# Quarters 1 to 3 of the first x block moved ahead of a runtime branch, in a macaron FFN, attention and convolution layer on 8 cores

## The chip, the cores and the metric

The kernel runs on all 8 cores of one Trainium2 chip. The time is the device time of the slowest core in microseconds (us), the median of the fast runs of a kernel. In some executions of any version the cores of one die (cores 0 to 3 or 4 to 7), sometimes of both, show a lower granted clock and the time is 2 to 19% longer; such runs are of the slow state and are left out of medians, means and ratios. "Same" is the class for a difference under 2%. Numbers of single cores come from profiled executions.

The program holds two bodies. The even cores (0, 2, 4, 6) run the first, by falling through a branch on a register; the odd cores (1, 3, 5, 7) take the branch to the second. An even core and the odd one after it are called a pair here.

## The reference, cut to what matters

Input x is 4 x 4096 x 1024, float32.

```python
def reference(x, ...):
    x = x + 0.5 * swiglu(rmsnorm(x, ffn1_norm), gate1, up1, down1)   # d_ff 2816
    z = rmsnorm(x, mix_norm) @ w_in                   # q, k, v (8 heads of 64) | a, b (512 each)
    attn = chunk_band_attention(q, k, v, rel_bias)    # 64-frame chunks, 576-key band
    conv = swish(layernorm(depthwise_conv31(a * sigmoid(b)) + dw_bias))
    x = x + concat(attn, conv) @ w_out
    x = x + 0.5 * swiglu(rmsnorm(x, ffn2_norm), gate2, up2, down2)
    return rmsnorm(x, final_norm)
```

(The comments are this text's shorthand.) Each core holds its share of the frames and works in two groups, group 0 and group 1, each through the whole layer.

## The kernel before

The kernel is written as a list scheduler: helpers such as `P.dma` append instructions and the waits they need to one list for each engine; the lists are replayed at the end. Estimated durations decide only the order.

The start. `load_x(G[0], 0, 4, some=...)` loads block 0 of x in quarters of 512 KB on the sync engine's queue:

```python
P.t["sp"] = 1.0
load_x(G[0], 0, 4, some=(0,))
P.dma("sp", lambda h: h.dma_start(out=cs[:, 0:CS_N], in_=cs_d), "cs0", ...)
P.first = P.E["sp"].items[:]          # what is in here goes out ahead of the branch
del P.E["sp"].items[:]
P.t["sp"] = 4.0
load_x(G[0], 0, 4, some=(1, 2, 3))    # in the body, behind the branch
tk = ("xl0_0_1", 16, "dma")           # quarter 1 has landed
P._need("pool", tk)                   # the gate: GpSimd's weight loads wait for it
for s, parts, m in ((2, 2, 2), (1, 4, 1)):
    issue_weights(ws["next"] + m)
    load_x(G[0], s, parts, eng="pool")
issue_weights()
# ... cut ...
for it in progs[0].first:
    it[1](nc.sync).then_inc(sems[it[2]], 16)
second = nc.values_load(half_d)
with nc.If(second == 0):
    body(progs[0])                    # even cores
with nc.Else():
    body(progs[1])                    # odd cores
```

The way of the convolution's input through HBM, in two halves r = 0 and 1 for each group. In the profile these are the store `gscr_0<-dreg` (group 1: `gscr_1<-dreg`) and the reload `dreg<-gscr_0`:

```python
def to_phases(g, r):
    P.dma("sp", ... out=gs_d[gi][r], in_=gTs[gi][:, r] ..., reads=(("g", gi, r),), writes=(("gs", gi, r),))
    P.dma("sp", ... out=gps[gi] ..., in_=gs_d[gi][r], reads=(("gs", gi, r),), ...)
    F.add(("gp", gi, r))
    hold["keys"] = (("gp", gi, m * r),)   # weight loads issued from here on wait for the reload
```

The softmax here doesn't subtract the row's maximum and nothing guards it: scores larger than these inputs give would overflow.

Of the kernel before, what the change touches and what calls it, by code (L numbers as in the profile page):

```python
# [283 lines left out]
def build_nc(debug=None):  # L284
# [20 lines left out]
    with ExitStack() as es:  # L305
# [81 lines left out]
        def make(half):  # L387
            P = Prog()
            plan = PLANS[half]
            G = [Group(i, b) for i, b in enumerate(plan)]  # L390
# [312 lines left out]
            def load_x(g, s, parts=1, eng="sp", some=None):  # L703
                n, c0 = g.n[s], g.off[s]
                w = 8 // parts
                for i in range(parts) if some is None else some:
                    lo, hi = 8 * c0 + i * w * n, 8 * c0 + (i + 1) * w * n
                    src = xin_d[g.gi, :, lo:hi]
                    wk = tuple(("x", g.gi, k, s) for k in range(i * w, (i + 1) * w))
                    P.dma(eng, lambda h, src=src, lo=lo, hi=hi: h.dma_start(out=xres[:, lo:hi], in_=src),  # L710
                          "xl%d_%d_%d" % (g.gi, s, i), 512 * w * n, writes=wk)
                F.add(("x", g.gi, s))
                if some == (0,):
                    return
                S.add(0, norm_load(g, s))
# [887 lines left out]
            P.t["sp"] = 1.0  # L1603
            load_x(G[0], 0, 4, some=(0,))
            P.dma("sp", lambda h: h.dma_start(out=cs[:, 0:CS_N], in_=cs_d), "cs0", 512 * CS_N, writes=("cs",), issue=0.45)
            P.first = P.E["sp"].items[:]
            del P.E["sp"].items[:]
            P.t["sp"] = 4.0
            load_x(G[0], 0, 4, some=(1, 2, 3))
            tk = ("xl0_0_1", 16, "dma")  # L1610
            P._need("pool", tk)
            P.t["pool"] = P.fin[tk[0:2]]
# [29 lines left out]
            return P  # L1642

        progs = [make(0), make(1)]
        sems = {}
        for nm in sorted(set(progs[0].sem_names()) | set(progs[1].sem_names())):
# [152 lines left out]
```

## Time and profile before

| | before |
|---|---|
| time | 1324.84 and 1324.96 us |
| spans, even cores 0, 2, 4, 6 | 1321.8, 1321.7, 1321.5, 1323.3 us |
| spans, odd cores 1, 3, 5, 7 | 1318.0, 1317.3, 1317.3, 1318.3 us |
| PE busy on core 6 | 1292.1 us, 98% |

The page of core 6 (the slowest), its busy time and the shares of the chain of work that ended last:

```profile
PE 1292.1 (98%) x8666; PEld 740.4 (56%) x8666; DVE 487.1 (37%) x899; ACT 407.0 (31%) x727; POOL 229.0 (17%) x266
...
PE 92%; DVE 3%; DMA 2%; issue 1%; ACT 1%; SPq 0%; DVEq 0%; POOL 0%; ACTq 0%; POOLq 0%
```

The kernel is bound by PE.

The chain of waits at the start of core 6 (start in us, duration, what; SPq is the sync engine's sequencer, L1673 its register load for the branch):

```profile
1.98 1.86 SPq L1673
...
4.47 3.73 DMA xres<-xin
...
8.81 7.63 DMA ring<-wgu
...
16.57 8.68 PE psA L561 x32
```

Read it downwards: quarters 1 to 3 of x go out only at 4.47 us, because the register loads stand in front of them; GpSimd's gate opens when quarter 1 has landed; the first weights need 7.63 us from issue to landing; then PE starts. The timeline of the same core has the same points as instructions (start, duration, engine, line, operation, tiles, count, and in brackets the idle time before and who ended it):

```profile
4.47 1.28 SPq L710 DMA_DIRECT2D xres<-xin  x3
...
8.81 2.29 POOL L668 DMA_DIRECT2D ring<-wgu  x4 [8.11 <-DMA xres<-xin]
...
16.57 5.23 PE L561 MATMUL psA<-dreg,ring 128*128 128x512 bf16 x16 [2.49 <-DMA ring<-wgu]
```

Here and below, a matmul is called warm when TensorE's granted clock is 1.00 and cold when it is near 0.5. This tile ran cold in part: its 16 matmuls took 5.23 us at a granted clock of 0.62 (16 to 18 us) and 0.53 (18 to 20 us), where core 0's took 3.62 us. PE had idled 2.49 us before it.

What the DMA engines of the two cores of a pair did at 8 to 10 us (the table of windows: the length of the stretch, then busy time and count of PE, PEld, DVE, ACT and POOL; the last three columns are the granted clock, the busy share of the core's 16 DMA engines and GB/s). Core 6 first, then core 7:

```profile
8.00:10.00 2.00, 2.00 (x11) 1.17 (x10) 1.16 (x3) 1.27 (x3) 1.19 (x2) 1.00 0.99 377
```

Core 1's timeline shows how late an odd core begins: GpSimd, ScalarE and VectorE execute the branch at 2.65 to 2.8 us (PE at 3.8, the sync engine at 4.3), but the first instruction of the body starts at 7.1, and x goes out then:

```profile
7.11 0.17 DVE L1602 MEMSET cb_sb<- 128x128 bf16 x1 [7.11 <-issue]
7.16 2.45 SPq L710 DMA_DIRECT2D xres<-xin  x3
...
13.69 2.58 POOL L668 DMA_DIRECT2D ring<-wgu  x4 [12.98 <-DMA xres<-xin]
```

Two loads of convolution weights go out at 311.14, the second store of the conv input at 311.86; the store has landed when its reload is issued, at 321.75:

```profile
311.14 1.08 POOL L668 DMA_DIRECT2D ring<-cwscr  x2 [27.13 <-DMA dreg<-gscr_0]
...
311.86 0.37 SPq L1080 DMA_DIRECT2D gscr_0<-dreg  x1
...
321.75 0.32 SPq L1085 DMA_DIRECT2D dreg<-gscr_0  x1
321.78 0.61 DVE L1295 TENSOR_TENSOR dreg<-ps,cs_sb 128x432 f32<-128x432 f32 x1 [3.82 <-PE ps L561]
...
322.54 1.89 PE L561 MATMUL ps<-at,hT 128*128 128x512 bf16 x8 [0.77 <-DVE dreg L1295]
```

VectorE's idle time is put down to PE, the last releaser by the record; but it starts 0.03 us after the reload is issued, so the store's landing released it. PE then idles 0.77 us.

### The profile page before, as it was taken

To read this page: it belongs to the slowest core of one execution; us is meant where nothing else is said; L and a number is where in the kernel's file an instruction comes from. 1 tells how busy PE (TensorE), PEld (TensorE's weight loads), DVE (VectorE), ACT (ScalarE), POOL (GpSimd) and SP (SyncE) were. 2 spreads that over 40 slices of the span, in tenths; PEclk is the share of its full clock that TensorE was granted. 3 is DMA by queue.
4 is the path that set the end of the run, shared out by engine and by line. 5 is a ranking of instruction groups with operands and counts; after the bars stand their busy time and mean duration, and the time that the engine had idled before them with its cause. 6 is when DMAs were issued, how large, how long until landed. Compare 5 with 4: busy or idle time off the path is not lost.

```text
span 1323.3 us, 23324 instructions; the slowest of 8 cores (1317.3 to 1323.3 us)
## 1 busy us (share of the span) xinstructions
PE 1292.1 (98%) x8666; PEld 740.4 (56%) x8666; DVE 487.1 (37%) x899; ACT 407.0 (31%) x727; POOL 229.0 (17%) x266
## 2 busy tenths in 40 slices
PE   7999999999999999999999999999999999999995
PEld 3655655566665666665564444446566664444444
DVE  4522222263745522222266222125455362222125
ACT  3411011242666421001236110114338661101123
POOL 2263000341003320000161000014120220000022
PEclk9999999999999999999999999999999999999998
DMA  8795226244930753243445844342784125433503
GB/s 187 164 217 116 49 47 120 42 127 142 193 70 2 188 91 72 53 76 53 73 52 101 218 80 82 66 76 49 171 208 103 34 39 111 75 65 64 112 0 130
DMA packets 33923, 129.55 MB, mean 98 GB/s; under 512 B 2832, under 2 KB 13200, under 8 KB 26896
## 3 DMA queue, kind: packets, MB, share of 16 engines
q0 software_dynamic: 18752, 97.33, 38.9%
q1 hardware_dynamic: 15056, 30.68, 6.8%
q8 instruction: 73, 1.20, 0.4%
q14 instruction: 42, 0.34, 0.1%
HBM read 193.54 MB, written 18.68 MB: 160 GB/s over the span
## 4 chain that ended last, share of the span: by engine, by line
PE 92%; DVE 3%; DMA 2%; issue 1%; ACT 1%; SPq 0%; DVEq 0%; POOL 0%; ACTq 0%; POOLq 0%
PE psA L561 53%; PE ps L561 39%; DVE hT L823 1%; DMA gscr_1<-dreg 1%; DMA ring<-wgu 1%; DVE xres L1048 1%; DVE xres L823 0%; DMA dreg<-gscr_1 0%; ACT L569 0%; DMA xres<-xin 0%; ACT rstd L574 0%; SPq L1673 0%; DVE xres L1556 0%; ACT pb L574 0%; POOL ssb L771 0%
## 5 line engine op out<-in xcount | busy, mean ns | idle before, releaser
L561 PE MATMUL psA<-hT,ring 128*128 128x512 bf16 (+2 forms) x3792 | 691.4, 344 | 1.7 <-DVE dreg L1139 1.0
L561 PEld LDWEIGHTS psA<-hT,ring 128*128 128x128 bf16 x3792 | 370.6, 98 | 316.1 <-issue 3.6
L574 ACT ACTIVATE dreg<-psA 128x512 f32<-128x512 f32 (+3 forms) x279 | 162.3, 587 | 688.1 <-PE psA L561 678.6
L561 PE MATMUL ps<-at,ring 128*128 128x512 bf16 (+2 forms) x1920 | 326.6, 332 | 0.0
L1014 DVE TENSOR_TENSOR at<-psA,dreg 128x512 bf16<-128x512 f32 (+2 forms) x213 | 130.1, 612 | 450.7 <-PE psA L561 427.3
L561 PEld LDWEIGHTS ps<-at,ring 128*128 128x128 bf16 x1920 | 187.6, 98 | 137.2
L1048 DVE SCALAR_TENSOR_TENSOR xres<-ps,xres 128x512 f32<-128x512 f32 (+2 forms) x160 | 88.5, 556 | 168.0 <-PE ps L561 168.0
L766 POOL TENSOR_TENSOR ssum<-ssum,sq 128x512 f32<-128x512 f32 (+2 forms) x102 | 103.2, 1012 | 169.4 <-ACT sq L574 165.6
L668 POOL DMA_DIRECT2D ring<-wgu x47 | 25.6, 546 | 522.9 <-PE ps L561 261.0
L561 PE MATMUL ps<-dreg,ring 128*128 128x256 bf16 (+4 forms) x704 | 85.7, 274 | 2.1 <-DMA dreg<-gscr_1 1.5
L574 ACT ACTIVATE sq<-xres 128x256 bf16<-128x256 f32 (+2 forms) x108 | 55.3, 519 | 99.8 <-DVE xres L1048 66.7
L823 DVE SCALAR_TENSOR_TENSOR hT<-xres,cs_sb,rstd 128x256 bf16<-128x256 f32 (+2 forms) x120 | 70.4, 644 | 12.4 <-ACT rstd L574 12.4
L561 PEld LDWEIGHTS ps<-dreg,ring 128*128 128x128 bf16 x704 | 55.2, 98 | 23.1 <-issue 4.4
L561 PE MATMUL ps<-hT,ring 128*128 128x512 bf16 (+2 forms) x352 | 63.4, 336 | 0.0
L561 PEld LDWEIGHTS ps<-hT,ring 128*128 128x128 bf16 x352 | 33.6, 98 | 25.5 <-issue 0.4
L569 ACT ACT_TABLE_LOAD x36 | 46.2, 1283 | 0.6
L574 ACT ACTIVATE pb<-psA 128x1024 bf16<-128x1024 f32 (+2 forms) x42 | 37.7, 915 | 8.1 <-PE psA L561 7.9
L1556 DVE TENSOR_TENSOR xres<-ps,xres 128x256 f32<-128x256 f32 (+2 forms) x48 | 24.9, 531 | 37.2 <-PE ps L561 37.1
L1576 POOL TENSOR_TENSOR dreg<-pb 128x2560 bf16<-128x2560 bf16 x8 | 35.8, 4502 | 0.7 <-DMA cwscr<-dreg 0.7
L668 POOL DMA_DIRECT2D ring<-wdA x16 | 8.6, 537 | 135.7 <-PE psA L561 135.3
L561 PE MATMUL ps<-at,hT 128*128 128x512 bf16 x136 | 30.8, 379 | 0.0
L561 PE MATMUL psA<-cb_sb 64*128 64x64 bf16 (+3 forms) x456 | 27.8, 223 | 0.0
(93 smaller groups left out, 588.5 us busy)
## 6 DMA issues: line engine op xcount, KB each, us to landing
ring<-wgu POOLq DMA_DIRECT2D x41, 1024.0 KB, 8.4
ring<-wdA POOLq DMA_DIRECT2D x16, 768.0 KB, 8.6
ring<-wdB POOLq DMA_DIRECT2D x16, 640.0 KB, 7.9
ring<-cwscr POOLq DMA_DIRECT2D x16, 640.0 KB, 9.7
cwscr<-dreg SPq DMA_DIRECT2D x8, 640.0 KB, 6.1
ring<-wab POOLq DMA_DIRECT2D x8, 512.0 KB, 8.2
ring<-wout POOLq DMA_DIRECT2D x4, 1024.0 KB, 14.7
dreg<-xin SPq DMA_DIRECT2D x2, 2048.0 KB, 21.9
```

Of the source, the lines that this page charges most:

```text
L561: P.op("pe", lambda h: h.matmul(o, lhsT=lhsT, rhs=rhs, start=start, stop=stop, skip_group_check=True), (max(n / 2400.0 + 0.0025, 0.03) if ...
L569: P.op("act", lambda h: h.activation(out=cs[0:1, CS_N + i:CS_N + i + 1], in_=onesS[0:1, 0:1], func=func), 1.5, ("cb1",), ())
L574: P.op("act", lambda h: h.activation(out=out, in_=in_, func=func, **kw), 0.12 + n / 1200.0 + (0.09 * sum(isinstance(v, bass.AP) for v in k ...
L668: P.dma("pool", lambda h, dst=dst, src=src: h.dma_start(out=dst, in_=src), wtok(p, i), (256 if p.reads else 512) * w, reads=p.reads, after ...
L766: pool(lambda h: h.tensor_tensor(out=ss, in0=ss, in1=sqt, op=ALU.add), n, (sk, ("sq", i)), (sk,))
L823: dve(lambda h, dst=dst, xin=xin, gcol=gcol: h.scalar_tensor_tensor(out=dst, in0=xin, scalar=gcol, in1=rt, op0=ALU.mult, op1=ALU.mult), n, ...
L1014: dve(lambda h: h.tensor_tensor(out=at, in0=ub, in1=tt, op=ALU.mult), n, (("ps", bU), ("tmpF", ti)), (("AT", gi, fl, s),))
L1048: dve(lambda h, xo=xo, xi=xi, bk=bk: h.scalar_tensor_tensor(out=xo, in0=bk, scalar=0.5, in1=xi, op0=ALU.mult, op1=ALU.add), n, (("ps", b), ...
L1556: dve(lambda h, xo=xo, bk=bk: h.tensor_tensor(out=xo, in0=bk, in1=xo, op=ALU.add), n, (("ps", b),) + rk, (("x", gi, dm, s),))
L1576: P.op("pool", lambda h, o_=o_, i0=i0: h.tensor_tensor(out=o_, in0=i0, in1=i1, op=ALU.mult), 4.5, ("cmp", "ic", "cb"), (("cwb", i % 2),))
```

## The change

Its intent: the sync queue is empty while the register loads and the branch run, so give it all of block 0 first. The gate stays on quarter 1.

```diff
             load_x(G[0], 0, 4, some=(0,))
             P.dma("sp", lambda h: h.dma_start(out=cs[:, 0:CS_N], in_=cs_d), "cs0", ...)
+            load_x(G[0], 0, 4, some=(1, 2, 3))
             P.first = P.E["sp"].items[:]
             del P.E["sp"].items[:]
             P.t["sp"] = 4.0
-            load_x(G[0], 0, 4, some=(1, 2, 3))
             tk = ("xl0_0_1", 16, "dma")
             P._need("pool", tk)
```

Both bodies share what is ahead of the branch, so the odd cores issue their x early as well.

## The prediction

> **What bounds the kernel now.** The page gives PE 98% busy and a chain of waits that is 92% PE: only the first tens of microseconds can move. The even cores take 1321.5 to 1323.3 us (core 6 is slowest), the odd ones 1317.3 to 1318.3: the even cores set the time.
>
> The start on core 6, by timeline and chain: the sync engine issues quarter 0 of x block 0 at 1.07 us and the constants at 1.52, spends 1.86 + 0.47 us on register loads, and issues quarters 1 to 3 only at 4.47. Quarter 0 lands at 5.0, quarter 1 at 8.2, quarter 3 about 11.2. GpSimd waits for quarter 1 (8.1 us) and issues the first weights at 8.81; their first half lands 7.63 us later, and the first real tile starts at 16.57, after 2.5 us of PE idling on that DMA. From there PE is nearly full, except where that GpSimd queue feeds it late (core 0: third weight piece at 32.4 us).
>
> In core 6's DMA records the hardware queue moves about 0.4 MB per us, and nothing from about 5 to 6 us: the hole that the change fills.
>
> **What the change does.** No work is added or removed. Three issues (1.28 us of the sync queue) move from 4.47 to about 2.0 us, before the branch. The sync engine branches 1.3 us later, which costs nothing (next task at 41 us); GpSimd loads its branch register itself.
>
> With the queue kept busy, quarter 1 lands at about 6.2 us (estimate: 1.1 MB at 0.4 MB per us from 2.0 us, plus about 1 us of latency and landing), quarter 3 at about 8.5. So the gate opens 2.0 to 2.5 us sooner on even cores, and the weight stream moves with it. Odd cores enter the branch at 6.6 to 7.9 us ([...] the trace has instruction packets there), quarter 1 lands at 13.1, and they gain 4 to 5 us, off the path.
>
> Given back: the odd weight stream starts about 2 us after the even one instead of 4.5, and while both run an even core's weights arrive at about 0.15 instead of 0.2 MB per us; that costs 0.5 to 0.8 us (estimate).
>
> The statistics of block 0 become bound by ScalarE (1.24 us per quarter) instead of DMA and end about 1.2 us earlier, so PE idles about 1.5 us before the first tile. [...] I expect it warm, which saves core 6 up to 1.6 us more.
>
> **Sum.** Even cores gain 1.5 us, core 6 about 2.5 to 3. Slowest span about 1320.7 us; time about 1322.8 us, range 1321.0 to 1324.8. Faster by over 2%: 1%; within 2%: 98%; slower: 1%.
>
> **What would show it.** Quarter 1's landing and the first weight issue at 6 to 7 us on even cores (8.81 before); first tile at 14.2 to 14.8 us in 3.6 us; odd cores ending 4 us sooner; the same instructions, apart from a few warm-up matmuls.
>
> **What would make it wrong.** x in flight holding up the odd cores' instruction fetch by several us; a cold first tile on some even core (+1.6 us); pair contention taking the whole shift, so that core 0 still waits for its third weight piece at 32 us; a schedule in another order; slow-state runs.

2.0 to 2.5 us at the gate less 0.5 to 0.8 us given back make about 1.5 us on the even cores, and core 6 adds up to 1.6 us (5.23 - 3.62), which was put at 2.5 to 3 in all. The trace of the kernel before has the numbers behind the estimates: 377 to 414 GB/s on cores 6 and 0 at 8 to 10 us; 1.02 us from core 6's first issue of x (1.07) to its first packet (2.09); and on core 6, while GpSimd loaded weights, 211 GB/s at 16 to 18 us and 152 to 164 at 18 to 24, when core 7 got 145 to 156.

## More of the kernel before

The convolution's accumulation, whose target lies over the buffer that the second store (r = 1) still reads, so that it waits for that store (L1295 in the profile of core 0's convolution stage of group 0):

```python
dve(lambda h, ...: h.tensor_tensor(out=a3, in0=b3, in1=bc, op=ALU.add), w, (("ps", b), "cs"), ak)
```

The convolution weights (`ring<-cwscr`, eight pieces of 640 KB for each group) come through GpSimd's queue.

```profile
8.00:10.00 2.00, 2.00 (x11) 1.35 (x10) 0.79 (x2) 1.25 (x3) 0.00 (x0) 1.00 0.55 111
```

Core 6 has its DMA engines nearly always busy and gets 377 GB/s, while its neighbour has just begun and gets 111.

## The result, and the profile after

| | before | changed kernel |
|---|---|---|
| median of the fast runs (3 and 4) | 1324.84 us (1323.6, 1324.84, 1324.96; one slow run, 1436.27, left out) | 1326.12 us (1324.52, 1325.28, 1326.95, 1329.01) |
| ratio of fast runs | | 1.0015, 95% interval 0.9991 to 1.0039: same |
| spans, even cores 0, 2, 4, 6 | 1321.8, 1321.7, 1321.5, 1323.3 | 1323.0, 1327.0, 1318.7, 1322.6 |
| spans, odd cores 1, 3, 5, 7 | 1318.0, 1317.3, 1317.3, 1318.3 | 1317.6, 1320.2, 1321.3, 1320.6 |

A ratio here is the mean time of one kernel's fast runs over that of the other's fast runs of the same rounds, so it is not quite the ratio of the medians quoted.

The time is in the predicted class, but outside the predicted range, on the side of no gain. And the even cores, which agreed within 2 us before, now spread over 8 us. The page of core 2, the slowest, has the chain nearly as before, with DMA at 3% instead of 2%:

```profile
PE 91%; DMA 3%; DVE 3%; issue 1%; ACT 1%; DVEq 0%; POOL 0%; SPq 0%; ACTq 0%; POOLq 0%
```

**The start of an even core.** The chain of waits at the start of core 6, then its timeline:

```profile
1.99 6.82 DMA xres<-xin
```

```profile
1.99 1.52 SPq L710 DMA_DIRECT2D xres<-xin  x3
...
9.42 2.31 POOL L668 DMA_DIRECT2D ring<-wgu  x4 [8.72 <-DMA xres<-xin]
...
15.18 3.61 PE L561 MATMUL psA<-dreg,ring 128*128 128x512 bf16 x15 [0.26 <-DMA ring<-wgu]
```

Quarters 1 to 3 go out 2.5 us sooner, as planned, but quarter 1 takes 6.82 us instead of 3.73, and the gate opens at 9.42 instead of 8.81. (The whole block is no sooner either: on the even cores its last quarter lands at 11.6 to 12.0 us, against 11.0 to 11.3 before.) PE still starts 1.4 us sooner on this core, warm, since from the weights' issue to the tile it takes 5.8 us (15.18 - 9.42) instead of 7.8 (16.57 - 8.81). Why the weights were faster is not shown; two things fit: when they went out, 0.46 MB of this core's x were still to land instead of 0.65, and the neighbour's x had landed by 12.6 us instead of 15.8. The windows of core 6 and then of core 7, 8 to 10 us, show why quarter 1 was slow:

```profile
8.00:10.00 2.00, 2.00 (x9) 1.02 (x7) 1.09 (x2) 1.71 (x3) 0.58 (x1) 1.00 0.94 287
```

```profile
8.00:10.00 2.00, 0.00 (x0) 0.00 (x0) 0.00 (x0) 0.00 (x0) 0.00 (x0) 1.00 0.96 291
```

Now both cores of the pair load at once, with their DMA engines about as busy (0.94 and 0.96), and core 6 gets 287 GB/s instead of 377, core 7 291. Over 4 to 6 us it was 277 and 243, over 6 to 8 us 242 and 152.

**The start of an odd core.** The chain of waits of core 1, then its timeline:

```profile
3.00 7.39 issue
...
10.41 3.69 issue
```

```profile
1.98 1.90 SPq L710 DMA_DIRECT2D xres<-xin  x3
10.50 0.17 DVE L1602 MEMSET cb_sb<- 128x128 bf16 x1 [10.50 <-issue]
...
14.10 2.29 POOL L668 DMA_DIRECT2D ring<-wgu  x4 [13.39 <-issue]
```

x goes out 5 us sooner than before, but the body starts 3.4 us later, at 10.50, and the first weights go out at 14.10 with "issue" ahead of them: nothing that the profile shows was waited for. GpSimd executed its branch at 2.95 us. What lies between fits its instruction fetch: in the raw DMA records the first packets of core 1's instruction queues after the start come at 4.3 us before the change and at 8.5 after it, when 1.3 of the 2.2 MB of x and constants have landed. On the even cores, which fall through the branch, there are none before 33.0 us in either kernel.

**The convolution stage of core 0**, the lines that answer to those shown above, and the chain's view of it:

```profile
308.56 1.08 POOL L668 DMA_DIRECT2D ring<-cwscr  x2 [25.86 <-PE psA L561]
...
310.55 0.37 SPq L1080 DMA_DIRECT2D gscr_0<-dreg  x1
...
321.64 0.32 SPq L1085 DMA_DIRECT2D dreg<-gscr_0  x1
321.67 0.61 DVE L1295 TENSOR_TENSOR dreg<-ps,cs_sb 128x432 f32<-128x432 f32 x1 [5.02 <-DMA gscr_0<-dreg]
...
322.43 2.48 PE L561 MATMUL ps<-at,hT 128*128 128x512 bf16 x8 [1.96 <-DVE dreg L1295]
```

```profile
310.55 11.03 DMA gscr_0<-dreg
```

The core came here 1.3 us sooner than before and left no sooner: the store takes 11.03 us instead of 9.9, PE idles 1.96 us instead of 0.77, and the 8 matmuls behind the gap take 2.48 us instead of 1.89, so PE was no longer warm (granted clock 0.50 from 324 to 326 us, 1.00 in the kernel before). The whole start gain is gone in this place.

**The sum.** I took fixed VectorE instructions as marks (they are the same in all kernels) and measured the stretches between them, named by their rough time in us. Between 60 and 300, 350 and 450, 450 and 945, 985 and 1050, and 1050 and 1300 us the even cores take the same time in every kernel whose order of work is the same, within 0.05 us, apart from 0.6 us more on three cores (core 2 of the kernel before is one) and 0.1 us in places. Beside that, only three quantities vary: the start (the time of the first mark, near 60 us), S1 (300 to 350, the convolution stage of group 0) and S2 (945 to 985, that of group 1). Odd cores vary at the start and by up to about 2 us elsewhere. Means of the four even cores of the profiled runs:

| us | start | S1 | S2 | sum |
|---|---|---|---|---|
| before | 60.19 | 49.60 | 41.70 | 151.49 |
| changed | 59.22 | 50.89 | 42.40 | 152.51 |
| difference | -0.97 | +1.29 | +0.70 | +1.02 |

(The even cores' spans differ by 0.75 us on average; the tail behind the last mark varies between 21.1 and 22.1 us, and the 0.6 us of core 2 before count too.) So in these two executions the start did gain 1 us, of the 1.5 predicted, and the two convolution stages took it back. S1 has a floor of 49.04 us, S2 one of 40.53. The largest single loss is core 2's S2, 45.45 us, which made it the slowest core. The critical chain of core 2, before and then after (the store's trip through the DMA engines, then the reload's):

```profile
945.50 7.84 DMA gscr_1<-dreg
...
953.61 3.76 DMA dreg<-gscr_1
```

```profile
946.68 9.38 DMA gscr_1<-dreg
...
956.33 4.80 DMA dreg<-gscr_1
```

PE waits for that reload, 0.56 us before and 3.13 us after, and then runs cold (granted clock 0.50 from 962 to 964 us):

```profile
961.26 5.15 PE L561 MATMUL ps<-dreg,ring 128*128 128x128 bf16 x60 [3.13 <-DMA dreg<-gscr_1]
```

### The profile page after: what moved, and what is told of

It reads as the page before. It is cut to its first block, busy times and chain, and to the rows that moved or that the text cites. A ratio compares the mean times of both kernels' runs of the same rounds, so it can differ in the third digit from the quotient of the medians.

```text
span 1327.0 us, 23308 instructions; the slowest of 8 cores (1317.6 to 1327.0 us)
## 1 busy us (share of the span) xinstructions
PE 1293.8 (97%) x8658; PEld 741.5 (56%) x8658; DVE 487.7 (37%) x899; ACT 407.3 (31%) x727; POOL 228.9 (17%) x266
## 4 chain that ended last, share of the span: by engine, by line
PE 91%; DMA 3%; DVE 3%; issue 1%; ACT 1%; DVEq 0%; POOL 0%; SPq 0%; ACTq 0%; POOLq 0%
PE psA L561 53%; PE ps L561 38%; DVE hT L823 1%; DMA gscr_0<-dreg 1%; DMA gscr_1<-dreg 1%; DMA ring<-wgu 1%; DMA xres<-xin 1%; DVE xres L1048 1%; DVE xres L823 0%; DMA dreg<-gscr_1 0%; ACT L569 0%; ACT rstd L574 0%; DVE xres L1556 0%; ACT pb L574 0%; POOL ssb L771 0%
```

## The experiments

**The question.** Is the loss of the changed kernel (a) only scatter between executions, or (b) made by the change, and if so by which part: the lower rate of x, the late odd cores, or what stands ahead of the store? "d" below is the start of the odd core of a pair minus that of its even core (the two bodies order their work differently, so the mark near 60 us is not the same instruction in both, and the zero of d is a convention: only differences of d mean something); before, it was -0.4 to -1.7 us in the profiled run; in the changed kernel -0.4, +1.2, +1.8 and +4.9. "Before" of a job is the kernel before, run alternately on the same chip.

### 1. The changed kernel once more

No edit. The changed kernel, 5 fast runs.

> The changed kernel once more, for spans of all cores in more runs. Theory A (the start on even cores is 1.1 to 1.4 us earlier, and the store of the conv stage at 310 to 322 us decides how much of that arrives): first tile on even cores at 15.1 to 15.4 us, DVE about 1.3 us ahead of before at 300 us, but at 330 us anywhere between 3 us ahead and 2 us behind; time 0 to 2 us over before. Rival B (the gain carries through and the slow profiled run was chance): time 1 to 1.5 us under before.

Measured: median 1323.91 us, against 1325.20 for the kernel before beside it; ratio 0.9987 (0.9974 to 1.0000). Even cores average 1321.32 us over the fast runs, against 1322.32 for the kernel before beside it. Profiled: start 59.6, S1 50.7, S2 41.1. So the 1326.1 of the first job was partly scatter: S1 was high again, S2 wasn't. As to time, theory A (0 to 2 us over before) was a miss and rival B (1 to 1.5 us under) was met, and the even cores gained 1.0 us here, about what the start gains: the take-back seen in the first job is not there in every run. (In that run d was -2.0, -0.7, +1.8 and +2.1, and S1 50.0, 50.6, 51.1 and 51.2 in this order.) Over both jobs the changed kernel has 9 fast runs with a mean of 1325.06 us ((4 x 1326.44 + 5 x 1323.96) / 9), against 1325.37 for the kernel before in the job of this run; the two jobs' ratios, 1.0015 and 0.9987, lie on either side of 1: no effect that these runs resolve.

### 2. The kernel before once more

No edit, one look; a first check that S1 and S2 vary in the unchanged kernel, too.

> The kernel before once more, for a second trace: even cores' stretch from 300 to 350 us again at 49 to 50.5 us if that is a property of the kernel and not of one run; odd cores entering the branch at 6.5 to 8.1 us; first tile at 16.1 to 16.6 us on even cores.

Measured: 1324.61 us; S1 50.03 to 50.40 on all four even cores, d -0.2 to -2.1, S2 40.53 to 41.18. As expected, and useful: in this run the kernel before is already 1 us above S1's floor (0.55 us in the first one).

### 3. Only quarter 1 ahead of the branch

```diff
-            load_x(G[0], 0, 4, some=(1, 2, 3))   # ahead of the branch
+            load_x(G[0], 0, 4, some=(1,))        # ahead
+            load_x(G[0], 0, 4, some=(2, 3))      # behind it
```

> Only quarter 1 is issued before the branch, quarters 2 and 3 stay behind it. Theory A says that quarter 1 landed at 9 us in the changed kernel because both cores of a pair loaded 2.2 MB at once at about 0.23 MB per us each, and that the odd cores' instruction fetch stood behind that x: with 1.1 MB in flight quarter 1 should land at 6 to 7 us on even cores, odd cores should enter the branch at 8 to 8.5 us (10.5 to 11.8 with three quarters, 7.1 to 8.1 with none) and issue weights before 10 us. Rival (three issues back to back delay the first, or the sync engine's later branch holds the others): quarter 1 at 8.5 to 9 us, or odd cores entering at 10 us or later. Time: 0 to 2 us under before.

Measured: median 1323.61 us; ratio 0.9987 (0.9974 to 0.9999). Quarter 1 is used at 6.7 to 8.1 us on the even cores, the first weights go out at 7.2 to 8.6, the first tile starts at 14.0 to 15.2. So the gate does open sooner when less x competes: the lower rate in the changed kernel came of the other quarters. How much of it came of the core's own and how much of its neighbour's this run doesn't separate. The odd cores enter the body at 8.4 to 9.8 us and send their first weights at 11.2 to 14.6, later than expected; with about 1 MB in flight, too, they enter later than before (7.1 us on core 1). The even cores start at 58.0, 2.1 us sooner than before, but S1 is 51.2 on average: the same take-back, larger. S2, though, is 40.6 here, 1.1 us below the kernel before, and over the fast runs the even cores are 1.6 us sooner (1320.69 against 1322.32 us): what the two stages do together differs from run to run.

### 4. The gate on quarter 3, order of the loads as before

```diff
-            tk = ("xl0_0_1", 16, "dma")
+            tk = ("xl0_0_3", 16, "dma")
```

> The kernel before with the weights waiting for quarter 3 instead of quarter 1: the whole start moves about 3 us later. If a shift of the start carries to the end one to one, time is 3 us over before (1327.5 to 1328.5). If the store of the conv stage absorbs shifts, as theory A has it, time is 0 to 2 us over before, with the difference in DVE progress at 300 us near +3 and smaller at 330 us.

Measured: median 1326.54 us; ratio 1.0006 (0.9993 to 1.0019). The gate opens at 11.7 us, 2.6 later, but the first tile starts only 1.1 us later, at 17.3 to 17.6: the tile follows the weights' issue after 5.7 us instead of 7.3. So 2.6 us at the gate cost about one at the first tile, which fits weights that, issued early, stand behind x in the DMA engines. The other direction is not shown by this run; in experiment 3 the gate opened 1.0 us sooner and the tile started 1.8 us sooner. S1 was 51.4 to 53.2 here, with d at 0.1 to 1.4.

### 5. Only the odd cores later, even program unchanged

Two kernels. In the first the odd cores' gate is on quarter 3; in the second they also wait for the landing of a later load (`cmp`).

```diff
-            tk = ("xl0_0_1", 16, "dma")
+            tk = ("xl0_0_%d" % (3 if half else 1), 16, "dma")
+            # second kernel only, if half: cmp is loaded here and GpSimd waits for it as well
```

> The kernel before; only the odd cores' weights wait for quarter 3 instead of quarter 1, so odd cores run about 2.2 us later from there on and nothing of the even cores' program changes. Theory C (what the even cores gain at the start is lost in their conv stage between 300 and 350 us, because the odd core of the pair comes later and its transfers then fall on the even core's store): odd minus even at 60 us goes from about -0.9 to about +1.3 us, that stretch on even cores from 49.0 to 50.3 us to 51 to 53 us, even spans up by 1 to 3 us, time 1 to 3 us over before. Rival D (the even cores' conv stage depends on their own timing alone, or on chance): that stretch 49 to 50.5 us, even spans and time the same as before within 0.5 us.

> As the run before it, with odd cores some 6 to 7 us later than in the kernel before (their weights wait for quarter 3 and then for one more transfer). Theory C: odd minus even at 60 us is about +6 us, past the collision, so the stretch from 300 to 350 us on even cores is back at 49 to 50.3 us and even spans are those of before within 0.5 us (the odd cores then take about as long as the even ones, 1323 to 1325 us, so the time itself may rise). If a later odd core simply hurts the even one: 52 us or more. Rival D: as before.

Measured, first: median 1326.23 us, ratio 1.0008 (0.9995 to 1.0021); on the pairs with d = 1.45 and 1.55 S1 is 51.1 and 51.0, at the low end of the 51 to 53 expected, and on those with d = -0.05 and 2.81 it is 50.7 and 49.7; the even cores' spans rose by 0.3 us (1322.70 against 1322.38), not by the 1 to 3 expected. Second: median 1327.15 us (the odd cores, held back to 1324.9, now set it), ratio 1.0014 (1.0001 to 1.0028); d is 4.8 to 8.1, S1 49.04 on three even cores and 49.47 on the fourth, S2 40.53 on all four. The even cores' spans average 1320.96 us against 1322.38 of the kernel before beside it. Core 0 of the second kernel, where the two loads still leave 2.2 us ahead of the store:

```profile
309.42 1.08 POOL L668 DMA_DIRECT2D ring<-cwscr  x2 [25.61 <-PE psA L561]
...
311.66 0.37 SPq L1080 DMA_DIRECT2D gscr<-dreg  x1
...
319.67 0.32 SPq L1085 DMA_DIRECT2D dreg<-gscr  x1
```

What follows: the even cores run the same program in both and yet gain 1.4 us or lose in S1, by nothing but when their neighbours run. So S1 depends on d, and the change moves d; that is how it can make the loss seen in the first job. How much of that loss is the change's and how much scatter, the two jobs of the changed kernel leave open. The even cores of all profiled runs of experiments 1 to 6, of the kernel before and of the changed one, ordered by the second store's trip (its issue to the issue of its reload):

| store's trip, us | seen at d | PE gap behind it | S1 |
|---|---|---|---|
| 6.9 to 8.9 | -0.7 and -1.7 (before, cores 2 and 6); +3.0 to +8.1 | none | 49.0 to 50.0 |
| 9.2 to 10.3 | -2.1 to 0.0, +0.8, +2.8 | 0.1 to 1.2 us | 49.7 to 50.7 |
| 10.4 to 11.4 | -0.7, and +0.1 to +2.1 | 1.3 to 2.3 us | 50.6 to 53.2 |

A neighbour at d = 0 to 2 us is the worst, and that is where the change puts half of the pairs (four of eight in its two profiled runs, at +1.2 to +2.1). In some runs with a gap of 1.96 us or more the next matmuls ran cold: on core 0 of the changed kernel, cold after 1.96 us, S1 was 52.85 us, and on its core 6, warm after 1.87 us, 51.57.

The traces show one part of how d acts. In all 36 cases of this table the two weight loads leave 0.77 us after the reload of the first half (r = 0) has landed, as `hold` demands. At d = -2.1 to -0.7 that reload takes 3.5 to 5.2 us, so that the loads leave up to 2.0 us ahead of the store or, on cores 2 and 6 before, with it; from d = -0.4 on it takes 3.3 to 3.6 us and the loads leave 1.7 to 2.4 us ahead, but for one case (4.7 us, 0.7 ahead).

### 6. One quarter ahead, and the odd cores later on purpose

```diff
# on top of "Only quarter 1 ahead of the branch"
-            tk = ("xl0_0_1", 16, "dma")
+            tk = ("xl0_0_%d" % (2 if half else 1), 16, "dma")
```

> Quarter 1 alone ahead of the branch, and odd cores' weights wait for quarter 2: even cores start 2 us early as with one quarter ahead, odd cores about 2 us later than there. Theory C: odd minus even at 60 us of 3 to 4 us, the stretch from 300 to 350 us on even cores 49 to 50.5 us instead of 50 to 53, even spans near 1319, odd spans 1318 to 1320.5, time near 1322 (3 us under before, 1 to 2 under one quarter ahead). Rival D: same as one quarter ahead, 1323.8.

Measured: median 1325.42 us, ratio 1.0003 (0.9990 to 1.0016). A miss: d was +0.3, +0.8, +1.8 and +4.7, so only one pair got the good phase (S1 49.99) and the others 50.5 to 51.1. The phase can't be set this way; it scatters by several us from pair to pair. The even cores' mean span was 1320.70 us, 1.7 below the kernel before, but the slowest core counts.

### 7. The scheduler told that the store takes longer

```diff
# to_phases, the store on the sync queue
-   reads=(("g", gi, r),), writes=(("gs", gi, r),), issue=0.6)
+   reads=(("g", gi, r),), writes=(("gs", gi, r),), issue=0.6, late=7.5)
```

> The kernel before with one number of the scheduler's own time estimates changed: the store of the conv stage is taken to land 5.5 us later than assumed (the trace has 10 us from issue to landing), so other matmuls are put where PE would wait for it. Theory A: the wait of DVE L1295 on that store (about 4 to 5 us of DVE idle, up to 2 us of PE idle) shrinks and PE runs on at full clock; time 1 to 4 us under before. If the store costs nothing on the path: time the same as before within 0.5 us.

Measured: median 1328.55 us, ratio 1.0022 (1.0009 to 1.0035): slower. The other estimate reorders PE's work in many places, so this says nothing about the store. From here on I added waits to the finished lists and left the order alone.

### 8. The store ahead of the weight loads, built wrongly

The theory by now: the second store stands in the DMA engines behind the two convolution weight loads that left up to 2.4 us earlier (1.3 MB), longer when the neighbour moves data too. Two of the fastest cases, before's cores 2 and 6, had those loads leave with the store instead of ahead of it. So I let them wait until VectorE has written what the store reads. Three kernels: the changed one, the one-quarter one, and the one before, each with this edit:

```diff
# issue_weights, even cores only
+   if half == 0 and p is wp[(0, "cv", 0)]:
+       P.late_at = len(P.E["pool"].items)
# to_phases
+   if half == 0 and (gi, r) == (0, 1):
+       P.late_tok = P.lastw[("g", 0, 1)]
# when the schedule is complete
+   P.E["pool"].items.insert(P.late_at, ("wait",) + P.late_tok[0:2])
```

> The changed kernel with one wait more, on even cores only, and no other instruction moved: GpSimd's two loads of the convolution weights in group 0 wait until VectorE has written what the second store of the conv input (gscr_0<-dreg) reads, so these loads leave no more than a fraction of a us before that store instead of about 2 us. Theory (the store waits in the DMA engines behind these 1.3 MB, longer while the odd neighbour moves data too; VectorE waits for the store, then PE): the store lands in 8.5 us or less on all even cores, no PE idle over 1.9 us behind it, the conv stretch of group 0 (S1, before 49.05 to 50.2, changed kernel 50.5 to 53) lasts 49.0 to 49.8 us whatever the phase of the neighbour; even cores end about 1.3 us sooner than the changed kernel's pooled mean (1322.1), near 1320.8; time about 1322.8. Rival A (the neighbour's traffic alone slows the store): S1 stays at 50.5 to 53 where the odd core starts 0 to 2 us after the even one; time 1324 to 1326. Rival B (the later loads now come late for PE): a new wait of PE on the convolution weights, S1 over 51 everywhere.

> The version with only quarter 1 ahead of the branch (1323.9 before), with the same added wait. Theory: S1 49.0 to 49.8 on every even core, with the first tile still at 14.0 to 15.2 us; even cores near 1319.3, time about 1321.5, which would beat both kernels by 2 to 4 us. Rival A: S1 as before in this version (mean 51.2), time 1323 to 1325. Rival B: S1 over 51 everywhere.

> The kernel before with the same added wait. Theory: S1 49.0 to 49.6, against 49.05 to 50.4 without it; even cores 0.6 us sooner, near 1321.7; time about 1324.7. The difference between this and the changed kernel with the same wait is then the change's gain at the start alone: 1 to 2 us in favour of the changed kernel. Rival A: S1 as before, no difference. Rival B: slower by 1 us or more.

Measured: medians 1334.38, 1331.65 and 1334.08 us; ratios 1.0065 (1.0051 to 1.0078), 1.0046 (1.0033 to 1.0060) and 1.0059 (1.0047 to 1.0072). The store's trip fell to 4.5 to 6.6 us with no gap of PE behind it, but S1 rose to 57.6 to 60.4. Core 0 of the third kernel:

```profile
314.67 3.29 POOL L670 DMA_DIRECT2D ring<-cwscr  x6 [30.49 <-DVE gh L1153]
...
323.38 4.96 PE L561 MATMUL ps<-dreg,ring 128*128 128x144 bf16 x40 [8.20 <-DMA ring<-cwscr]
```

"x6" shows the mistake: pieces 0 to 3 had long been loaded at this point in the kernels without the edit, and the two that go out beside the store are pieces 4 and 5. I had held up six loads, and PE waited 8.2 us for the first ones. The expected rival B (loads late for PE) is what happened, by an error of mine and not by the idea; the store's half of the theory held.

### 9. The same with the right two loads

```diff
-   if half == 0 and p is wp[(0, "cv", 0)]:
+   if half == 0 and p is wp[(0, "cv", 4)]:
```

The instruction lists of GpSimd differ from those without the edit in one wait, and those of the other engines in nothing.

> The changed kernel with one wait more, on even cores only, and no other instruction moved: the two loads of ring<-cwscr that go out just ahead of the second gscr_0<-dreg store (the fifth and sixth pieces; e8 put the wait on the first piece by mistake and held up six) wait until VectorE has written what that store reads, so they leave with the store (12.6 to 13.7 us after the marker instead of 10.3 to 12.6). Theory: the store lands in 8.5 us or less, no PE idling over 1.9 us behind it, S1 49.0 to 49.8 whatever the neighbour's phase (changed kernel 50.5 to 53), S2 as before; even cores near 1320.8, time about 1322.8. Rival A (the neighbour's traffic alone slows the store): S1 50.5 to 53 where the odd core starts 0 to 2 us later; time 1324 to 1326. Rival B (these two loads come late for PE): PE waits for ring<-cwscr and S1 is over 51 everywhere.

> The version with only quarter 1 ahead of the branch (1323.9), with the same added wait. Theory: S1 49.0 to 49.8 on every even core, even cores near 1319.3, time about 1321.5, which would beat both kernels. Rival A: S1 51 on average as without the wait, time 1323 to 1325. Rival B: S1 over 51 everywhere.

> The kernel before with the same added wait. Theory: S1 49.0 to 49.6 (49.05 to 50.4 without), even cores 0.5 us sooner, time about 1324.8; the distance of the changed kernel with the same wait to this one is then the gain of the change at the start alone, 1 to 2 us. Rival A: no difference to before. Rival B: slower by 1 us or more.

| with the wait, based on | median us | ratio (interval) | even cores' mean span | S1 on the four even cores | d |
|---|---|---|---|---|---|
| changed kernel | 1323.56 | 0.9985 (0.9972 to 0.9999) | 1320.43 | 49.04, 49.04, 49.04, 49.05 | -0.1 to +1.9 |
| one quarter ahead | 1323.40 | 0.9990 (0.9976 to 1.0004) | 1320.52 | 49.05, 49.04, 49.04, 49.05 | -3.0 to +0.4 |
| kernel before | 1324.00 | 0.9989 (0.9976 to 1.0003) | 1321.22 | 49.04, 49.04, 49.20, 49.04 | -3.5 to -0.7 |
| (before, no wait) | 1325.23 | | 1322.08 | | |

S1 is at its floor on eleven of twelve cores, at every d seen (-3.5 to +1.9), and the store's trip is 4.9 to 6.7 us. Core 0 of the first kernel, with d = +1.9, the phase that had cost 51 to 53 us:

```profile
311.80 0.37 SPq L1082 DMA_DIRECT2D gscr<-dreg  x1
...
312.56 1.08 POOL L670 DMA_DIRECT2D ring<-cwscr  x2 [28.61 <-DVE at L1193]
...
316.89 0.32 SPq L1089 DMA_DIRECT2D dreg<-gscr  x1
```

What follows: the store waited behind this core's own two loads; rival A (the neighbour's traffic alone) is refuted, since the neighbours run as before. That the neighbour only made that queue longer is the reading that fits both experiments; it is not shown by itself. With the wait the change is worth about what it gains at the start: 1320.43 against 1321.22 us on the even cores, 0.8 us, against 0.9 at the first mark (59.3 and 60.3 us). On the time the two differ by 0.4 us, which 5 fast runs each don't resolve. The first and third came within 0.8 us of the times expected (1322.8 and 1324.8); the one-quarter version missed its 1321.5, for its start was 59.2 us, not the 58.0 of experiment 3, and its S2 41.1 to 41.9.

### 10. The same for group 1

S2 follows the trip of the first gscr_1 store in much the same manner in the two kernels and those of experiments 1 to 6 and 9: 5.3 to 7.4 us gives 40.5 to 40.9 us, 9.65 us gives 45.45 (core 4 of the changed kernel, 6.25 us and 41.61, is an exception). The kernels of experiment 8 don't fit: seven of their twelve even cores have 41.0 to 42.3 us at trips of 5.1 to 7.2 us. Ahead of it stand loads issued 14 to 18 us earlier (5.8 MB by the code's sizes: wv, wq and four pieces of convolution weights). On top of the first kernel of experiment 9, the third and fourth of those pieces wait in the same way.

> e11 with one wait more of the same kind in group 1, even cores only: the third and fourth ring<-cwscr loads there wait until VectorE has written what the first gscr_1<-dreg store reads; no other instruction is moved. In all kernels so far the stretch S2 follows that store's landing: 5.3 to 7.4 us to its reload gives 40.53 to 40.9, 7.5 to 8.2 gives 40.8 to 41.9, 8.6 gives 42.2, 9.65 gives 45.45. Theory (the store stands behind this core's own loads): first trip under 7 us, S2 40.5 to 40.7 on all even cores (e11: 40.5 to 41.9), even cores 0.7 us sooner than e11, near 1319.7, time about 1322.8. Rival A (it stands behind the neighbour's traffic or behind the loads left in front of it): trip and S2 as in e11. Rival B (the two loads come late): PE waits for ring<-cwscr, S2 over 42.

Measured: 1322.57, 1323.51 and 1323.69 us; ratio 0.9984 (0.9966 to 1.0003); even cores 1319.81 us. The store's trip fell to 5.3 to 5.5 us on all four cores, as expected, but S2 stayed at 40.9 to 41.4, which was not: the two loads, it seems, now stand in front of the reload. Core 0's critical chain:

```profile
943.77 5.05 DMA gscr<-dreg
...
949.08 6.64 DMA dreg<-gscr
```

The reload takes 6.2 to 6.6 us on the four cores instead of the 3.5 to 4.8 seen without the edit. So the first half of the theory (the store stands behind this core's own loads) holds in group 1 as well. That no order of store, reload and weights would do better there is not shown: this was the only one tried.

## Why the prediction was right or wrong, point by point

- **"What bounds the kernel", "even cores set the time", "within 2%": right.** PE 91 to 92% of the chain in both; even cores slowest in both.
- **"The same instructions", "the sync engine branches later, which costs nothing", "I expect it warm": right,** though the sync engine branched 3.9 us later on core 6 (8.24 instead of 4.37), not 1.3. Core 6's first tile went from 5.23 to 3.61 us. Three of the four even cores started it at 15.1 to 15.4 us, core 2 at 17.4 (15.6 to 17.0 in experiment 1).
- **"Quarter 1 lands at about 6.2 us (estimate: 1.1 MB at 0.4 MB per us)": wrong, by nearly 3 us, and this is the first step that failed.** The rate was read while the neighbour stood at its branch. The change lets both cores load 2.2 MB at once, and core 6 then gets 242 to 287 GB/s; quarter 1 landed at 8.8 to 9.2 us. The gate opened at 9.4 to 9.8 us, no sooner than before. Of the predicted 1.5 us about 1.0 came all the same, by another way than the predicted one: the gate was no sooner, but the weights arrived faster behind it. That much is luck.
- **"Odd cores ... gain 4 to 5 us, off the path": wrong.** Their first tile came at 21.0 to 24.0 us instead of 20.5 to 21.6. The first packets of their instruction queues come at 8.5 us instead of 4.3 (core 1), while the DMA engines are busy with x. I had listed this under what would make it wrong, and yet used the opposite in the sum. In "off the path" lay the greater mistake.
- **"Given back: ... 0.5 to 0.8 us (estimate)", of weights at the start: the wrong place and, in the first job, less than half of what was lost.** The give-back comes at 300 and 945 us: in the first job's profiled runs +1.3 us in S1 and +0.7 in S2, in the later ones (experiments 1 and 2) +0.5 and +0.1. The neighbour's phase d went from about -1 us to between +1 and +2 on half of the pairs, and in that phase the second conv store, which stands behind two weight loads of its own core, lands about 1 us later; PE waits for it, and on core 0 of the changed kernel ran cold behind it (granted clock 0.50). For S2 the cause is not shown to the same degree: the store there stands behind this core's own loads, but making it faster did not bring S2 to its floor (experiment 10). Experiment 5 shows the phase at work with an even program that isn't changed at all; experiment 9 shows the two loads as the cause, since one wait removes the loss in S1 at every phase seen.
- **The time.** 1326.1 in the first job, 1323.9 in the second, 1322.8 predicted. So part of the distance in the first job is scatter. I had given a range of 3.8 us; S1 and S2 each spread by 4 to 5 us over the cores and kernels seen here, and the slowest of four even cores is what counts. The profile before already had them 0.6 and 1.2 us above their floors, and I had taken the middle of the kernel as fixed because PE was "nearly full" there.

The version of experiment 9 based on the changed kernel is faster than the one before by 0.15% (the interval, 0.9972 to 0.9999, only just leaves out no effect). It was not run beside the changed kernel, whose second job had 1323.91 us, so that a gain over that one is not shown on the time; the one of experiment 10 is not told apart from it.

What stays open: why exactly a neighbour at d = 0 to 2 us is the worst (beyond the moment at which the loads leave, which of its transfers meet the store), why the weights behind the gate came faster, why d scatters by 2 to 5 us between pairs of one run, and where S2's remaining 1 us could go.

## What to carry to other kernels

A load moved forward is worth what the DMA engines can do with it at that moment: measure the rate with the neighbour core loading, too (core 6 got 377 GB/s at 8 to 10 us before and 287 with both loading), and look for what else has to pass the same engines (here instruction packets, too, came at 8.5 us instead of 4.3 on core 1, and its body started at 10.5 instead of 7.1). When a small gain at the start vanishes, cut the run into stretches at fixed instructions and compare the stretches, core by core: here those that varied in unchanged code, S1 (49.0 to 53.2 us) and S2 (40.5 to 45.45), held a wait that a transfer's landing decided. A store that another engine waits for should leave ahead of bulk loads that have time; here a single added wait in the finished schedule did it, worth 1.2 us alone and 1.7 with the change by the medians (the interval of the wait alone still touches no effect), where changing the scheduler's estimate cost about 3.

## What the traces and runs show of the hardware

- After the branch: in the kernel before, VectorE of the odd cores entered its body 3.2 to 4.7 us after the branch; on the even cores, which fall through, it had begun at 3.4 to 4.0. With 2.2 MB of x and constants in flight on each core of the pair the entry went from 7.1 to 10.5 us on core 1, with 1.1 MB (experiment 3) to 8.4 to 9.8 us on the odd cores.
- One register load of the sync engine took 1.82 us on core 1, and 3.84 us with x in flight; on GpSimd of that core it was 0.72 to 1.02 us.
- Rates of a pair: before the change, at 8 to 10 us, core 6 got 377 GB/s at a DMA share of 0.99 while its neighbour got 111, and core 0 got 414 while its neighbour got 43. With both loading, core 6 got 242 to 287 between 4 and 10 us, at shares of 0.94 to 1.02, for 512 KB loads on the sync queue.
- A store of the sync engine took 7.2 to 11.4 us behind two 640 KB loads of GpSimd, and 4.9 to 6.7 us when these were made to leave just after it (experiment 9).
- Cold matmuls were seen after some gaps of PE and not after others about as long: after 1.96 us 8 matmuls of 512 columns took 2.48 us instead of 1.89, and the granted clock was 0.50 from 324 to 326 us (changed kernel, core 0); after 2.49 us it was 0.62 and 0.53 (before, core 6, from 16 to 20 us); after 2.44 and 2.51 us it stayed at 1.00 (before, core 4 at 16.5 us and core 3 at 21.6). No run here shows what decides it.
